# A dilated convolution: a shared middle-tap product, clipped columns, casting loads, stores from SyncE

## Chip, cores, metric

One core of one Trainium2 chip. The metric is the device time of one execution in microseconds (us). "Ratio" is the mean time of one kernel's fast runs over the mean of the kernel before's fast runs of the same rounds, so it is not quite the ratio of the medians quoted. Some runs fall in a slower state, in which the same kernel takes over 1.5% longer; all runs compared here are in the fast state unless said otherwise. A tile is a buffer on the chip; PSUM is the memory that TensorE writes its results to.

## The reference

```python
batch, c_in, h, w, c_out, k, dilation = 16, 64, 64, 64, 128, 3, 2   # x, weight: f32
x_pad = np.pad(x, ((0, 0), (0, 0), (2, 2), (2, 2)))
output[b, co] += weight[co, ci, kh, kw] * x_pad[b, ci, kh*2:kh*2+h, kw*2:kw*2+w]
```

So 16.8 MB of f32 images come in and 33.5 MB of f32 results go out. Output row r needs input rows r-2, r, r+2.

## The kernel before

Two images are worked on at once: their 64 input channels sit on partitions 0-63 and 64-127, and a pair of matmuls (one for each image) runs side by side on the two row halves of TensorE. Each output tile is 8 rows of 64 columns (512 numbers), and takes nine pairs, one for each tap. The parts that matter:

```python
    def emit_input_dma(pb):                      # f32 into a staging tile, from SyncE
        x32 = x32pool.tile([P, H, W], f32, tag="x32")
        for lo, hi in (chunk_rows0 if pb == 0 else chunk_rows):
            nc.sync.dma_start(out=x32[:, lo:hi], in_=x_pair[pb, :, lo:hi])
    def emit_cast(pb, lo, hi, engine):           # to f16 with 2 zero columns on each side
        ...  nc.vector.tensor_copy(out=x3[:, lo:hi, pad:pad+W], in_=x32[:, lo:hi, :])   # or nc.scalar.copy
    def conv_matmul(x3, ps, ti, t, hb, first, last):
        ...  # rows above or below the image are left out, columns are not
        rhs = x3[hb*CI:(hb+1)*CI, lo+dh:hi+dh, pad+dw:pad+dw+W]
        nc.tensor.matmul(out=po, lhsT=lhsT, rhs=rhs, start=first, stop=last)
    ...
        for ti in range(ntiles):                 # 8 tiles of 8 rows, 8 image pairs
            for t in range(ntaps):               # 9
                for hb in range(2):
                    conv_matmul(x3, ps, ti, t, hb, t == 0, t == ntaps - 1)
            ...  # ScalarE and VectorE copy one PSUM tile each into o_sb
            ...  # every 4th tile: nc.gpsimd.dma_start(out=out_img[...], in_=o_sb...)   1 MB each
```

## Time and profile before

| | before |
|---|---|
| time, median | 142.72 us (142.18 to 143.32, 4 runs) |
| span in the profile | 140.7 us |
| convolution matmuls, first start to last end | 10.6 to 134.2 us |
| last data packet of a store | 138.0 us |

Lines of the page of the kernel before: busy time by engine; busy tenths and GB/s in 40 slices of the span; the DMA queues (packets, MB, time of their packets as a share of 16 DMA engines).

```profile
span 140.7 us, 2777 instructions
...
PE 125.1 (89%) x1170; PEld 71.5 (51%) x1170; DVE 55.7 (40%) x85; ACT 53.8 (38%) x86; POOL 21.4 (15%) x49
...
PE   0049999999999999999999999999999999999910
...
DMA  4999999999999999999999999892929385799970
GB/s 97 296 415 418 415 401 414 344 428 418 424 422 422 428 417 425 429 411 424 425 424 423 422 421 428 354 414 121 426 100 431 165 356 245 298 395 402 388 307 8
...
q0 software_dynamic: 4816, 31.61, 54.3%
q1 hardware_dynamic: 5904, 18.88, 34.6%
```

TensorE is full from the fourth slice to the 38th. The DMA (16 engines that move the data in packets) is full as well, but only until about slice 26; the holes behind it (121, 100, 165 GB/s) say that DMA had time to spare. The two large queues together are 89% of the span, 125 us: the second limit lies right behind the first.

The same by stretches (columns: stretch, its length, busy us and count of instructions of each engine, granted clock, DMA share, GB/s):

```profile
core 0: us, PE busy (x) PEld busy (x) DVE busy (x) ACT busy (x) POOL busy (x), PEclk, DMA share, GB/s
30.00:60.00 30.00, 30.00 (x288) 17.18 (x285) 13.17 (x20) 12.45 (x21) 4.21 (x8) 1.00 1.02 423
100.00:110.00 10.00, 10.00 (x99) 5.80 (x96) 4.15 (x6) 3.35 (x6) 1.05 (x2) 1.00 0.75 312
```

Between 30 and 60 us loads and stores together move 423 GB/s at a share of 1.02 (60 to 90: 418): that is a full DMA (the share sums the times of packets, so packets that overlap bring it over 1). From 90 to 120 us, when the loads have run out, stores alone leave a quarter or more of it idle.

The timeline in the middle of the kernel, TensorE only (start us, length us, engine and what):

```profile
60.11 0.38 PE L133 MATMUL ps_732<-x_sb_78,w_sb 64*128 64x512 f16 x1
...
60.33 0.38 PE L133 MATMUL ps_732<-x_sb_78,w_sb 64*128 64x512 f16 x1
...
60.54 0.38 PE L133 MATMUL ps_732<-x_sb_78,w_sb 64*128 64x512 f16 x1
```

A new pair starts every 0.215 us (60.11, 60.33, 60.54): 512 columns, with nothing between. Nothing that leaves the matmul work as it is can shorten the stretch from 10.6 to 134.2 us.

### The profile page before, as it was taken

Reading aid. Unit: us, or ns where it says so; the run is one execution under the profiler, and the core shown is the slowest. Engines: PE = TensorE matmul, PEld = TensorE weight load, DVE = VectorE, ACT = ScalarE, POOL = GpSimd, SP = SyncE. Lnnn points to the kernel's source line nnn. Section 1 sums busy time; section 2 is a strip of 40 time slices with the busy share of each in tenths; the row PEclk is TensorE's granted clock in tenths of the full one; section 3 lists DMA queues with packets and bytes.
Section 4 is the critical chain, followed back from the end, with each engine's and each line's share of the span. In section 5 each row is a group of like instructions: output and inputs, shape, how many; then the busy total and the mean of one; then the engine's idle time right before and its main releaser. Section 6 shows DMA issues by size and latency. Waiting matters only on the chain.

```text
span 140.7 us, 2777 instructions
## 1 busy us (share of the span) xinstructions
PE 125.1 (89%) x1170; PEld 71.5 (51%) x1170; DVE 55.7 (40%) x85; ACT 53.8 (38%) x86; POOL 21.4 (15%) x49
## 2 busy tenths in 40 slices
PE   0049999999999999999999999999999999999910
PEld 0035555655555555655565555555565556555500
DVE  0134556535353534445353435333233333323310
ACT  3144465652535343533635253532233333322310
POOL 6000003020202020201102030202020110433210
PEclk9999999999999999999999999999999999999985
DMA  4999999999999999999999999892929385799970
GB/s 97 296 415 418 415 401 414 344 428 418 424 422 422 428 417 425 429 411 424 425 424 423 422 421 428 354 414 121 426 100 431 165 356 245 298 395 402 388 307 8
DMA packets 10733, 50.66 MB, mean 360 GB/s; under 512 B 1248, under 2 KB 1376, under 8 KB 7136
## 3 DMA queue, kind: packets, MB, share of 16 engines
q0 software_dynamic: 4816, 31.61, 54.3%
q1 hardware_dynamic: 5904, 18.88, 34.6%
q8 instruction: 9, 0.15, 0.4%
q14 instruction: 4, 0.03, 0.1%
HBM read 17.07 MB, written 33.55 MB: 360 GB/s over the span
## 4 chain that ended last, share of the span: by engine, by line
PE 73%; issue 12%; DMA 5%; POOL 3%; SPq 1%; ACT 1%; POOLq 0%
DMA x_87<-in_x_dram 5%; POOL out_dram L185 3%; PE ps_134 L133 1%; PE ps_1378 L133 1%; PE ps_1327 L133 1%; PE ps_1235 L133 1%; PE ps_1163 L133 1%; PE ps_1114 L133 1%; PE ps_1020 L133 1%; PE ps_972 L133 1%; PE ps_923 L133 1%; PE ps_829 L133 1%; PE ps_781 L133 1%; PE ps_732 L133 1%; PE ps_638 L133 1%
## 5 line engine op out<-in xcount | busy, mean ns | idle before, releaser
L133 PEld LDWEIGHTS <-w_sb 64*128 64x128 f16 x1152 | 70.2, 94 | 53.1 <-issue 1.1
L113 PE MATMUL wt_95<-ident,w_70 128*64 128x128 f16 x1 | 0.4, 377 | 7.7 <-DMA w_70<-in_weight_dram 7.7
L185 POOL DMA_DIRECT2D out_dram<-o_sb_1471 x8 | 4.3, 541 | 10.4 <-DVE o_sb_1471 L177 5.3
L100 DVE CAST x_sb_78<-x_87 128x640 f16<-128x640 f32 (+2 forms) x3 | 1.8, 606 | 8.9 <-DMA x_87<-in_x_dram 8.9
L113 PEld LDWEIGHTS <-w_70 128*64 128x64 f16 x9 | 1.1, 209 | 7.7 <-DMA w_70<-in_weight_dram 7.7
L185 POOL DMA_DIRECT2D out_dram<-o_sb_131 x2 | 1.1, 548 | 23.1 <-ACT o_sb_131 L180 19.3
L102 ACT CAST x_sb_78<-x_87 128x512 f16<-128x512 f32 (+1 forms) x2 | 1.7, 830 | 6.4 <-DMA x_87<-in_x_dram 6.4
L133 PE MATMUL ps_133<-x_sb_78,w_sb 64*128 64x512 f16 (+1 forms) x9 | 3.4, 557 | 0.0
L133 PE MATMUL ps_134<-x_sb_78,w_sb 64*128 64x512 f16 (+1 forms) x9 | 3.2, 528 | 0.0
L185 POOL DMA_DIRECT2D out_dram<-o_sb_898 x2 | 1.1, 532 | 13.1 <-ACT o_sb_898 L180 13.1
L185 POOL DMA_DIRECT2D out_dram<-o_sb_516 x2 | 1.1, 531 | 13.1 <-ACT o_sb_516 L180 13.1
L185 POOL DMA_DIRECT2D out_dram<-o_sb_707 x2 | 1.1, 531 | 13.1 <-ACT o_sb_707 L180 13.1
L185 POOL DMA_DIRECT2D out_dram<-o_sb_1089 x2 | 1.1, 531 | 13.1 <-ACT o_sb_1089 L180 13.1
L185 POOL DMA_DIRECT2D out_dram<-o_sb_325 x2 | 1.1, 531 | 13.1 <-DVE o_sb_326 L181 13.1
L185 POOL DMA_DIRECT2D out_dram<-o_sb_1280 x2 | 1.1, 531 | 12.8 <-ACT o_sb_1280 L180 12.8
L102 ACT CAST x_sb_84<-x_391 128x1024 f16<-128x1024 f32 (+1 forms) x2 | 2.0, 992 | 2.6 <-DMA x_391<-in_x_dram 2.6
L102 ACT CAST x_sb_81<-x_200 128x1024 f16<-128x1024 f32 (+1 forms) x2 | 2.0, 990 | 2.6 <-DMA x_200<-in_x_dram 2.6
L102 ACT CAST x_sb_78<-x_582 128x1024 f16<-128x1024 f32 (+1 forms) x2 | 2.0, 994 | 1.4 <-PE ps_255 L133 1.4
L100 DVE CAST x_sb_84<-x_391 128x1152 f16<-128x1152 f32 (+1 forms) x2 | 1.5, 727 | 2.4 <-DMA x_391<-in_x_dram 2.4
L102 ACT CAST x_sb_81<-x_773 128x1024 f16<-128x1024 f32 (+1 forms) x2 | 2.0, 993 | 0.9 <-PE ps_423 L133 0.9
L102 ACT CAST x_sb_78<-x_1155 128x1024 f16<-128x1024 f32 (+1 forms) x2 | 2.0, 994 | 0.9 <-PE ps_805 L133 0.9
L102 ACT CAST x_sb_81<-x_1346 128x1024 f16<-128x1024 f32 (+1 forms) x2 | 2.0, 994 | 0.9 <-PE ps_996 L133 0.9
(309 smaller groups left out, 373.2 us busy)
## 6 DMA issues: line engine op xcount, KB each, us to landing
out_dram<-o_sb_131 POOLq DMA_DIRECT2D x2, 1024.0 KB, 10.3
out_dram<-o_sb_132 POOLq DMA_DIRECT2D x2, 1024.0 KB, 13.0
out_dram<-o_sb_325 POOLq DMA_DIRECT2D x2, 1024.0 KB, 11.1
out_dram<-o_sb_326 POOLq DMA_DIRECT2D x2, 1024.0 KB, 14.3
out_dram<-o_sb_516 POOLq DMA_DIRECT2D x2, 1024.0 KB, 11.1
out_dram<-o_sb_517 POOLq DMA_DIRECT2D x2, 1024.0 KB, 14.4
out_dram<-o_sb_707 POOLq DMA_DIRECT2D x2, 1024.0 KB, 10.8
out_dram<-o_sb_708 POOLq DMA_DIRECT2D x2, 1024.0 KB, 13.4
```

What stands on the lines that cost most here:

```text
L100: nc.vector.tensor_copy(out=x3[:, lo:hi, pad : pad + W], in_=x32[:, lo:hi, :])
L102: nc.scalar.copy(out=x3[:, lo:hi, pad : pad + W], in_=x32[:, lo:hi, :])
L113: nc.tensor.matmul(out=wt_ps[0:CI, 0:CO], lhsT=w_slice, rhs=ident)
L133: nc.tensor.matmul(out=po, lhsT=lhsT, rhs=rhs, start=first, stop=last)
L185: nc.gpsimd.dma_start(out=out_img[2 * pb, :, e0:e1], in_=o_sb0[:, e0:e1])
```

## The change

The intent: rows are taken in blocks of four. With a = rows 4b, 4b+1 and c = rows 4b+2, 4b+3 (c' the same of the block above, a' of the block below) and W0, W1, W2 the three rows of taps, output rows a need W1·a + W2·c + W0·c', and output rows c need W1·c + W0·a + W2·a'. The product W1·(a + c) is made once and added to both; the rest becomes (W2 - W1)·c + W0·c' and (W0 - W1)·a + W2·a'. That is five products instead of six. Side taps work on the 62 columns that exist. GpSimd's software queue casts f32 to f16 while loading, so the f32 staging and the casts on VectorE and ScalarE go. Stores are issued by SyncE; the instruction order is by hand.

```diff
-            nc.sync.dma_start(out=x32[:, lo:hi], in_=x_pair[pb, :, lo:hi])
-            nc.vector.tensor_copy(out=x3[:, lo:hi, pad : pad + W], in_=x32[:, lo:hi, :])
+        nc.gpsimd.dma_start(out=x16_tiles[pb][...], in_=x_pair[pb, :, lo:hi])      # f32 -> f16, 16-row chunks
+        nc.vector.tensor_tensor(out=s, in0=v[:, :, 0], in1=v[:, :, 1], op=add)      # rowsum: a + c
...
-            for t in range(ntaps):
-                for hb in range(2):
-                    conv_matmul(x3, ps, ti, t, hb, t == 0, t == ntaps - 1)
+            o0, o1 = max(0, -dw), W - max(0, dw)                                     # clipped columns
+        product(psP, sv, 0, 0, NBLK, True, True)                                     # W1 (a + c)
+        product(psA, blocks(x16, b0, NBLK, 1), 1, 0, NBLK, True, False)              # (W2 - W1) c
+        product(psA, blocks(x16, b0 + z - 1, NBLK - z, 1), 2, z, NBLK - z, False, True)   # W0 c'
+        product(psB, blocks(x16, b0, NBLK, 0), 3, 0, NBLK, True, False)              # (W0 - W1) a
+        product(psB, blocks(x16, b0 + 1, NBLK - z, 0), 4, 0, NBLK - z, False, True)  # W2 a'
...
-                nc.vector.tensor_copy(out=o_sb0[:, sl], in_=ps[0])
-                nc.scalar.copy(out=o_sb1[:, sl], in_=ps[1])
+        nc.scalar.copy(out=p_sb, in_=psP)
+        for e, ps in ((0, psA), (1, psB)):
+            nc.vector.tensor_tensor(out=o[...], in0=ps..., in1=pv, op=add)
...
-                nc.gpsimd.dma_start(out=out_img[2 * pb, :, e0:e1], in_=o_sb0[:, e0:e1])
+                nc.sync.dma_start(out=out_img[2 * pb + m, :, e0:e1], in_=o_tiles[pb][...])
... (weights cast and subtracted on VectorE/ScalarE, pools and order left out)
```

A "group" below is 16 rows of two images: 15 matmul pairs where there were 18.

More of the change, by code (lines that the diff above doesn't have):

```diff
@@ L22 @@
     CO, CI_w, KH, KW = weight.shape
-    assert CI == CI_w
-    d = 2 if isinstance(dilation, bass.AP) else int(dilation)
-    assert KH == KW == 3
-    assert CI == 64 and CO == 128
+    assert CI == CI_w == 64 and CO == 128
+    assert KH == KW == 3 and H == W == 64
     assert B % 2 == 0
+    assert not isinstance(dilation, bass.AP) and int(dilation) == 2
+    d = 2
     P = 128
-    pad = d
-    WP = W + 2 * pad
-    HW = H * W
     f32 = mybir.dt.float32
     f16 = mybir.dt.float16
-    ROWS = 512 // W
@@ L38 @@
-    ntiles = H // ROWS
-    assert H % ROWS == 0
-    NB = ROWS * W
-    CR = 2 * ROWS
-    nchunks = ntiles // 2
-    chunk_rows = [(0, CR + d)]
-    for c in range(1, nchunks - 1):
-        chunk_rows.append((c * CR + d, (c + 1) * CR + d))
-    chunk_rows.append(((nchunks - 1) * CR + d, H))
-    assert nchunks == 4
-    chunk_rows0 = [(0, ROWS + d), (ROWS + d, CR + d)] + chunk_rows[1:]
-    taps = [(0, 0)]
-    for kh in range(KH):
-        for kw in range(KW):
-            dh = (kh - KH // 2) * d
-            dw = (kw - KW // 2) * d
-            if (dh, dw) != (0, 0):
-                taps.append((dh, dw))
@@ L58 @@
-    ntaps = len(taps)
+    add = mybir.AluOpType.add
+    sub = mybir.AluOpType.subtract
+    HW = H * W
+    GR = 16
+    NG = H // GR
+    NBLK = GR // 4
+    NH = GR // 2 * W
     npairs = B // 2
-    NXB = 3
+    ngroups = npairs * NG
+    chunk_rows = [(g * GR + (d if g else 0), min((g + 1) * GR + d, H)) for g in range(NG)]
+    LOOK = 3
+    XB = 10
     wpool = ctx.enter_context(tc.tile_pool(name="wpool", bufs=1))
-    x32pool = ctx.enter_context(tc.tile_pool(name="x32pool", bufs=2))
-    xpool = ctx.enter_context(tc.tile_pool(name="xpool", bufs=1))
@@ L66 @@
-    opool = ctx.enter_context(tc.tile_pool(name="opool", bufs=4))
-    cpool = ctx.enter_context(tc.tile_pool(name="cpsum", bufs=8, space=bass.MemoryType.PSUM))
-    w16 = wpool.tile([CO, CI * KH * KW], f16, name="w16")
-    nc.gpsimd.dma_start(out=w16, in_=weight.rearrange("o i h w -> o (i h w)"))
+    xpool = ctx.enter_context(tc.tile_pool(name="xpool", bufs=5))
+    opool = ctx.enter_context(tc.tile_pool(name="opool", bufs=3))
+    spool = ctx.enter_context(tc.tile_pool(name="spool", bufs=3))
@@ new lines, with load @@
+    ppool = ctx.enter_context(tc.tile_pool(name="ppool", bufs=1, space=bass.MemoryType.PSUM))
+    apool = ctx.enter_context(tc.tile_pool(name="apool", bufs=3, space=bass.MemoryType.PSUM))
+    x_pair = x.rearrange("(nb two) c h w -> nb (two c) h w", two=2)
+    out_img = out.rearrange("b o h w -> b o (h w)")
+    x16_tiles = {}
+    xs_tiles = {}
+    def load(c):
+        pb, g = divmod(c, NG)
+        lo, hi = chunk_rows[g]
+        if g == 0:
+            x16_tiles[pb] = xpool.tile([P, HW], f16, tag="x16", name="x16")
+            xs_tiles[pb] = xpool.tile([P, HW // 2], f16, tag="xs", name="xs")
+        nc.gpsimd.dma_start(
+            out=x16_tiles[pb][:, lo * W : hi * W].rearrange("p (h w) -> p h w", w=W),
+            in_=x_pair[pb, :, lo:hi],
+        )
@@ new lines, in rowsum @@
+    def rowsum(c):
+        pb, g = divmod(c, NG)
+        v = x16_tiles[pb][:, g * GR * W : (g + 1) * GR * W].rearrange(
+            "p (b e q) -> p b e q", e=2, q=2 * W
+        )
+        s = xs_tiles[pb][:, g * NH : (g + 1) * NH].rearrange("p (b q) -> p b q", q=2 * W)
+        nc.vector.tensor_tensor(out=s, in0=v[:, :, 0], in1=v[:, :, 1], op=add)
+    ctx.enter_context(tc.manual_schedule())
+    w32 = wpool.tile([CO, CI * KH * KW], f32, name="w32")
+    nc.scalar.dma_start(out=w32, in_=weight.rearrange("o i h w -> o (i h w)"))
@@ L72 @@
     ident = wpool.tile([P, P], f16, name="ident")
     make_identity(nc, ident)
-    w_sb = wpool.tile([P, ntaps * CO], f16, name="w_sb")
-    x3_bufs = []
-    for i in range(NXB):
-        x_sb = xpool.tile([P, H * WP], f16, tag=f"xsb{i}", name=f"x_sb{i}")
-        x3 = x_sb.rearrange("p (h w) -> p h w", w=WP)
-        nc.gpsimd.memset(x3[:, :, 0:pad], 0.0)
-        nc.gpsimd.memset(x3[:, :, pad + W :], 0.0)
-        x3_bufs.append(x3)
-    x_pair = x.rearrange("(nb two) c h w -> nb (two c) h w", two=2)
@@ L86 @@
-    out_img = out.rearrange("b o h w -> b o (h w)")
-    x32_tiles = {}
-    def emit_input_dma(pb):
-        x32 = x32pool.tile([P, H, W], f32, tag="x32")
-        x32_tiles[pb] = x32
-        for lo, hi in (chunk_rows0 if pb == 0 else chunk_rows):
-            nc.sync.dma_start(out=x32[:, lo:hi], in_=x_pair[pb, :, lo:hi])
-    def emit_cast(pb, lo, hi, engine):
-        x3 = x3_bufs[pb % NXB]
-        x32 = x32_tiles[pb]
-        if engine == "v":
-            nc.vector.tensor_copy(out=x3[:, lo:hi, pad : pad + W], in_=x32[:, lo:hi, :])
-        else:
-            nc.scalar.copy(out=x3[:, lo:hi, pad : pad + W], in_=x32[:, lo:hi, :])
@@ L104 @@
-    emit_input_dma(0)
-    emit_cast(0, chunk_rows0[0][0], chunk_rows0[0][1], "v")
-    emit_cast(0, chunk_rows0[1][0], chunk_rows0[1][1], "s")
-    for t, (dh, dw) in enumerate(taps):
-        kh = dh // d + KH // 2
-        kw = dw // d + KW // 2
-        w_slice = w16.rearrange("o (i k) -> o i k", k=KH * KW)[:, :, kh * KW + kw]
-        wt_ps = cpool.tile([CO, NB], f32, tag="ps", name=f"wt{t}")
-        nc.tensor.matmul(out=wt_ps[0:CI, 0:CO], lhsT=w_slice, rhs=ident)
-        nc.tensor.matmul(out=wt_ps[CI : 2 * CI, 0:CO], lhsT=w_slice, rhs=ident)
-        dst = w_sb[:, t * CO : (t + 1) * CO]
-        if t % 2 == 0:
-            nc.scalar.copy(out=dst, in_=wt_ps[:, 0:CO])
-        else:
-            nc.vector.tensor_copy(out=dst, in_=wt_ps[:, 0:CO])
@@ L121, in conv_matmul @@
-    def conv_matmul(x3, ps, ti, t, hb, first, last):
-        dh, dw = taps[t]
-        r0 = ti * ROWS
-        lo = max(r0, -dh)
-        hi = min(r0 + ROWS, H - dh)
-        lhsT = w_sb[hb * CI : (hb + 1) * CI, t * CO : (t + 1) * CO]
-        rhs = x3[
-            hb * CI : (hb + 1) * CI,
-            lo + dh : hi + dh,
-            pad + dw : pad + dw + W,
-        ]
-        po = ps[hb][:, (lo - r0) * W : (hi - r0) * W]
-        nc.tensor.matmul(out=po, lhsT=lhsT, rhs=rhs, start=first, stop=last)
@@ L135 @@
-    for pb in range(npairs):
-        x3 = x3_bufs[pb % NXB]
-        o_sb0 = opool.tile([P, HW], f32, tag="osb")
-        o_sb1 = opool.tile([P, HW], f32, tag="osb")
-        first_pair = pb == 0
-        last_pair = pb == npairs - 1
-        if last_pair:
-            flush_after = {ti: (ti * NB, (ti + 1) * NB) for ti in range(ntiles)}
-        else:
-            flush_after = {
-                ntiles // 2 - 1: (0, HW // 2),
-                ntiles - 1: (HW // 2, HW),
-            }
-        for ti in range(ntiles):
-            ps = [
-                cpool.tile([CO, NB], f32, tag="ps", name=f"ps{hb}") for hb in range(2)
-            ]
-            for t in range(ntaps):
-                for hb in range(2):
-                    conv_matmul(x3, ps, ti, t, hb, t == 0, t == ntaps - 1)
-            if first_pair:
-                if ti == 0:
-                    emit_cast(0, chunk_rows[1][0], chunk_rows[1][1], "v")
-                    emit_cast(0, chunk_rows[2][0], chunk_rows[2][1], "s")
-                elif ti == 1:
-                    emit_cast(0, chunk_rows[3][0], chunk_rows[3][1], "v")
-            if pb + 1 < npairs:
-                if ti == 2:
-                    emit_input_dma(pb + 1)
-                elif ti == 4:
-                    emit_cast(pb + 1, chunk_rows[0][0], chunk_rows[0][1], "v")
-                    emit_cast(pb + 1, chunk_rows[1][0], chunk_rows[1][1], "s")
-                elif ti == 5:
-                    emit_cast(pb + 1, chunk_rows[2][0], chunk_rows[2][1], "v")
-                    emit_cast(pb + 1, chunk_rows[3][0], chunk_rows[3][1], "s")
-            sl = slice(ti * NB, (ti + 1) * NB)
-            if ti % 2 == 0:
-                nc.vector.tensor_copy(out=o_sb0[:, sl], in_=ps[0])
-                nc.scalar.copy(out=o_sb1[:, sl], in_=ps[1])
-            else:
-                nc.scalar.copy(out=o_sb0[:, sl], in_=ps[0])
-                nc.vector.tensor_copy(out=o_sb1[:, sl], in_=ps[1])
-            if ti in flush_after:
-                e0, e1 = flush_after[ti]
-                nc.gpsimd.dma_start(out=out_img[2 * pb, :, e0:e1], in_=o_sb0[:, e0:e1])
-                if last_pair:
-                    nc.sync.dma_start(
-                        out=out_img[2 * pb + 1, :, e0:e1], in_=o_sb1[:, e0:e1]
-                    )
-                else:
-                    nc.gpsimd.dma_start(
-                        out=out_img[2 * pb + 1, :, e0:e1], in_=o_sb1[:, e0:e1]
-                    )
@@ new lines @@
+    for c in range(XB):
+        if c < ngroups:
+            load(c)
+    KINDS = 5
+    wd = wpool.tile([CO, KINDS * KW * 2 * CI], f16, name="wd")
+    wdv = wd.rearrange("o (k j r i) -> o k j r i", k=KINDS, j=KW, r=2)
+    wv = w32.rearrange("o (i h w) -> o h w i", h=KH, w=KW)
+    for r in range(2):
+        nc.vector.tensor_copy(out=wdv[:, 0, :, r], in_=wv[:, 1])
+        nc.vector.tensor_tensor(out=wdv[:, 1, :, r], in0=wv[:, 2], in1=wv[:, 1], op=sub)
+        nc.vector.tensor_tensor(out=wdv[:, 3, :, r], in0=wv[:, 0], in1=wv[:, 1], op=sub)
+        nc.scalar.copy(out=wdv[:, 2, :, r], in_=wv[:, 0])
+        nc.scalar.copy(out=wdv[:, 4, :, r], in_=wv[:, 2])
@@ new lines @@
+    w_sb = wpool.tile([P, KINDS * KW * CO], f16, name="w_sb")
+    NT = KINDS * KW
+    for q in range(0, NT, 8):
+        n = min(8, NT - q)
+        wt = apool.tile([P, 1024], f32, tag="ab", name="wt")
+        for t in range(q, q + n):
+            nc.tensor.matmul(
+                out=wt[:, (t - q) * CO : (t - q + 1) * CO],
+                lhsT=wd[:, t * 2 * CI : (t + 1) * 2 * CI],
+                rhs=ident,
+            )
+        h = n // 2 * CO
+        nc.vector.tensor_copy(out=w_sb[:, q * CO : q * CO + h], in_=wt[:, 0:h])
+        nc.scalar.copy(out=w_sb[:, q * CO + h : (q + n) * CO], in_=wt[:, h : n * CO])
@@ new lines, in product @@
+    def product(ps, src, kind, blk0, nblk, first, last):
+        for j in (1, 0, 2):
+            dw = (j - 1) * d
+            o0, o1 = max(0, -dw), W - max(0, dw)
+            t = kind * KW + j
+            for hb in range(2):
+                pp = slice(hb * CI, (hb + 1) * CI)
+                rhs = src(pp, dw + o0, dw + o1)
+                po = ps[:, hb * NH + blk0 * 2 * W : hb * NH + (blk0 + nblk) * 2 * W]
+                po = po.rearrange("p (r w) -> p r w", w=W)[:, :, o0:o1]
+                nc.tensor.matmul(
+                    out=po,
+                    lhsT=w_sb[pp, t * CO : (t + 1) * CO],
+                    rhs=rhs,
+                    start=first and j == 1,
+                    stop=last and j == 2,
+                )
@@ new lines, in blocks, with prepare @@
+    def blocks(x16, b0, n, e):
+        v = x16.rearrange("p (b e r w) -> p b e r w", e=2, r=2, w=W)
+        return lambda pp, c0, c1: v[pp, b0 : b0 + n, e, :, c0:c1]
+    ahead = [0]
+    def prepare(n):
+        while ahead[0] < min(n, ngroups):
+            c = ahead[0]
+            rowsum(c)
+            if c + XB < ngroups:
+                load(c + XB)
+            ahead[0] += 1
+    prepare(2)
+    o_tiles = {}
+    for G in range(ngroups):
+        pb, g = divmod(G, NG)
+        x16 = x16_tiles[pb]
+        xs = xs_tiles[pb].rearrange("p (r w) -> p r w", w=W)
+        if g == 0:
+            o_tiles[pb] = opool.tile([P, 2 * HW], f32, tag="osb", name="osb")
+        o = o_tiles[pb].rearrange("p (m b e q) -> p m b e q", m=2, e=2, q=2 * W)
+        b0 = g * NBLK
+        psP = ppool.tile([P, 2 * NH], f32, tag="p", name="psP")
+        sv = lambda pp, c0, c1: xs[pp, g * GR // 2 : (g + 1) * GR // 2, c0:c1]
+        product(psP, sv, 0, 0, NBLK, True, True)
+        psA = apool.tile([P, 2 * NH], f32, tag="ab", name="psA")
+        product(psA, blocks(x16, b0, NBLK, 1), 1, 0, NBLK, True, False)
+        z = 1 if g == 0 else 0
+        product(psA, blocks(x16, b0 + z - 1, NBLK - z, 1), 2, z, NBLK - z, False, True)
+        psB = apool.tile([P, 2 * NH], f32, tag="ab", name="psB")
+        product(psB, blocks(x16, b0, NBLK, 0), 3, 0, NBLK, True, False)
+        z = 1 if g == NG - 1 else 0
+        product(psB, blocks(x16, b0 + 1, NBLK - z, 0), 4, 0, NBLK - z, False, True)
+        p_sb = spool.tile([P, 2 * NH], f32, tag="psb", name="p_sb")
+        nc.scalar.copy(out=p_sb, in_=psP)
+        pv = p_sb.rearrange("p (m b q) -> p m b q", m=2, q=2 * W)
+        for e, ps in ((0, psA), (1, psB)):
+            nc.vector.tensor_tensor(
+                out=o[:, :, b0 : b0 + NBLK, e],
+                in0=ps.rearrange("p (m b q) -> p m b q", m=2, q=2 * W),
+                in1=pv,
+                op=add,
+            )
+        prepare(min(2 * G + 4, G + 1 + LOOK))
+        if g % 2 == 1:
+            e0, e1 = (g - 1) * GR * W, (g + 1) * GR * W
+            for m in range(2):
+                nc.sync.dma_start(
+                    out=out_img[2 * pb + m, :, e0:e1],
+                    in_=o_tiles[pb][:, m * HW + e0 : m * HW + e1],
+                )
```

## The prediction

> **What bounds the kernel now.** TensorE does. In the timeline a pair of convolution matmuls (two images on the two row halves, 512 columns) starts every 0.216 us, from 10.6 to 134 us without a gap; the page's part 1 has PE busy 125.1 us of a span of 140.7. The last stores end 6.5 us later. Right behind stands the DMA: page part 3 gives its two large queues 54.3% and 34.6% of the span, 125 us together; the slices show it full until about 85 us (423 GB/s), with holes only after the loads have run out.
>
> **What the change does.**
> - TensorE: per 16 rows 15 pairs for 18, and side taps of 62 columns for 64. Columns per image pair fall 19%, from 36,096 to 29,328. At the 0.216 us per 512 columns of the trace the convolution takes 99-100 us (3.1 us per 16-row group) for 123. I expect no penalty for 62-column rows.
> - Casts leave VectorE and ScalarE, about 25 us each. VectorE gets per group two PSUM additions of 1,024 and a row sum of 512. The trace's 512-element PSUM copy took 0.692 us, 0.53 of it streaming; I estimate 2.65 us per group, 85 us in all: below TensorE. ScalarE: one copy of 1,024, about 1.0 us.
> - DMA: HBM bytes stay, 17.07 MB in and 33.55 out. Stores move to SyncE, which buys no bandwidth: the Trainium skill ("DMA: Bandwidth & Descriptors", "Issuing engines are not separate DMA queues") says all issuers share 16 engines, and the packet records agree: 4 KB rows take 159-162 ns on either queue. An 8 KB store row takes 309 ns; 256 such per engine are 79 us. For the cast there is one sample: the weights (2,304 B read, 1,152 written per row) took 106 ns a row. A plain row of that size would take about 93 by the other rows (9 ns + 27.3 B/ns). So a cast is charged for the bytes it reads, plus 12-15%. Plain 4 KB load rows take 159 ns; cast I estimate 171-183, so 44-47 us for all loads.
>
> **Critical path.** DMA work becomes 79 + 44..47 + about 2 (weights, semaphores, instruction fetch) = 125-128 us, more than TensorE's 99-100: the bound moves to DMA, and only part of the 23 us is collected. The first x packet comes later: GpSimd issues it after the identity, about 1.9 us, and that queue's first packet came 2.8 us after its issue in before, so at 4.7 us; before, loads began at 1.8. The DMA ends near 130 us; plus 2.7 us of ending as in before and 2 us between span and time: about **134.5 us**, range 128 to 139.5.
>
> Chances: over 2% faster 0.87, within 2% 0.10, slower 0.03.
>
> **What would show it.** DMA nines from slice 2 to the end; the software queue shows about 8.5 MB (it counts written bytes) yet 31-35% of the span, the hardware queue 33.6 MB and 58%; the last matmul ends near 110 us, then 15-20 us of pure stores; matmul pairs at about 0.21 us; cast rows of 2 KB at 171-183 ns; the chain ends in DMA.
>
> **What would make it wrong.** A cast cheaper than its read bytes (written-byte cost: about 125 us) or much dearer (over 140). Strided 62-column PSUM rows slowing matmuls by over 20%. Loads starved by 8 KB store rows, or the three output buffers stalling VectorE, so that TensorE ends late and DMA idles.

## The result, and the profile after

130.77 us median (130.54 to 130.93, 4 runs), before 142.72; ratio 0.9169 (95% interval 0.9131 to 0.9208). The prediction was 134.5 us with a range of 128 to 139.5.

The page of the changed kernel (parts 1 to 4, the lines that answer to those above, and the chain):

```profile
span 129.1 us, 2299 instructions
...
PE 103.4 (80%) x975; PEld 53.8 (42%) x975; DVE 91.4 (71%) x104; ACT 36.7 (28%) x39; POOL 17.7 (14%) x38
...
PE   0469999999999999999999999999999998000000
...
DMA  3999999999999999999999999999999999999980
GB/s 101 147 183 173 204 208 263 348 344 362 333 346 350 351 346 335 348 349 343 354 335 345 346 358 346 342 342 353 364 405 430 416 432 419 432 427 427 432 353 38
...
q1 hardware_dynamic: 4608, 33.56, 63.2%
q0 software_dynamic: 4608, 8.39, 35.9%
...
PE 79%; DVE 3%; DMA 2%; DVEq 1%; issue 0%
```

DMA nines now run to slice 38 without a hole, and TensorE stops at slice 34. With the weights' queue (0.7%) and the two instruction queues (0.3%) the page's queues sum to 100% of the span. Note the GB/s line: the page counts a casting load by the bytes that it writes, half of those that it reads. A slice with 345 GB/s, 69 of them cast, reads and writes 414.

```profile
core 0: us, PE busy (x) PEld busy (x) DVE busy (x) ACT busy (x) POOL busy (x), PEclk, DMA share, GB/s
30.00:60.00 30.00, 30.00 (x296) 15.62 (x292) 26.35 (x30) 9.80 (x10) 4.22 (x8) 1.00 1.05 345
110.00:120.00 10.00, 0.00 (x0) 0.00 (x0) 0.72 (x1) 0.00 (x0) 0.00 (x0) 0.58 1.01 428
```

TensorE stays full while it works (30.00 of 30 us), DMA too (share 1.05). From 110 us on, only stores run, at 428 GB/s.

The timeline in the middle, matmuls merged by tile:

```profile
40.18 1.23 DVE L190 TENSOR_TENSOR osb<-psA,p_sb 128x1024 f32<-128x1024 f32 x1 [0.42 <-PE psA L136]
41.16 0.81 PE L136 MATMUL psP<-xs,w_sb 64*128 64x512 f16 x6
41.38 1.23 DVE L190 TENSOR_TENSOR osb<-psB,p_sb 128x1024 f32<-128x1024 f32 x1
...
42.52 0.41 DVE L87 TENSOR_TENSOR xs<-x_174 128x512 f16<-128x512 f16 x1
...
44.34 0.81 PE L136 MATMUL psP<-xs,w_sb 64*128 64x512 f16 x6
```

psP starts at 41.16 and the next psP at 44.34: a group takes 3.17-3.18 us for 15 pairs, 0.211 us a pair. VectorE's two additions and the row sum fill 2.8 of them (1.23 + 1.22 + 0.42, the second following the first by 1.20).

The chain of waits, last pieces (start, length, what):

```profile
106.99 1.28 PE psA L136 x12
108.37 1.23 DVE osb L190
109.59 1.13 DVEq L236
```

The last matmul ends at 109.4 us; the chain ends with VectorE's last addition at 110.7 us and gives TensorE 79% of the span. But the span ends at 129.1 us. The 18 us in between are stores that nothing but the end of the program waits for, and the chain does not follow them. Which of the two pictures bounds the kernel is the first thing that the experiments asked.

The balance of the change in the two profiles: the convolution begins 2.7 us earlier (7.9 for 10.6) and is 22.1 us shorter (101.5 for 123.6), so the last matmul ends 24.8 us earlier (109.4 for 134.2). After the last matmul come 19.7 us for 6.5, so 13.2 us are given back. 24.8 - 13.2 = 11.6 us, the difference of the spans (140.7 - 129.1).

The packet records of the trace, which the page sums up, in medians of one data packet and in bytes counted at the source:

| | before | after |
|---|---|---|
| x row of 16 image rows: read -> written, ns | 4,096 -> 4,096 B: 159 | 4,096 -> 2,048 B: 172 |
| store row 8,192 B, ns | 309 | 322 beside casts, 309 alone |
| first x packet, us | 1.76 | 2.87 |
| GB/s read and written, 30-60 us | 423 | 414 |
| GB/s read and written, 5-15 us | 409-414 | 366 |
| last data packet, us | 138.0 | 127.4 |
| span end after it, us | 2.7 | 1.7 |

### The profile page after: what moved, and what is told of

The parts are those of the page before. It is cut to its first block, busy times and chain, and to the rows that moved or that the text cites. A ratio compares the mean times of both kernels' runs of the same rounds, so it can differ in the third digit from the quotient of the medians.

```text
span 129.1 us, 2299 instructions
## 1 busy us (share of the span) xinstructions
PE 103.4 (80%) x975; PEld 53.8 (42%) x975; DVE 91.4 (71%) x104; ACT 36.7 (28%) x39; POOL 17.7 (14%) x38
## 3 DMA queue, kind: packets, MB, share of 16 engines
q1 hardware_dynamic: 4608, 33.56, 63.2%
q0 software_dynamic: 4608, 8.39, 35.9%
## 4 chain that ended last, share of the span: by engine, by line
PE 79%; DVE 3%; DMA 2%; DVEq 1%; issue 0%
PE psA L136 31%; PE psB L136 30%; PE psP L136 16%; DMA w_75<-in_weight_dram 2%; PE wt L116 1%; DVE osb L190 1%; DVEq L236 1%; DVE wd L105 1%; DVE w_sb L122 0%; DVE wd L107 0%; DVE wd L106 0%; DVE xs L87 0%; DVEq L190 0%
## 5 line engine op out<-in xcount | busy, mean ns | idle before, releaser
L136 PEld LDWEIGHTS <-w_sb 64*128 64x128 f16 x960 | 52.3, 95 | 50.0 <-issue 3.0
L187 ACT COPY p_sb<-psP 128x1024 f32<-128x1024 f32 x32 | 32.4, 1012 | 67.6 <-PE psP L136 67.6
L190 DVE TENSOR_TENSOR osb<-psA,p_sb 128x1024 f32<-128x1024 f32 x32 | 39.2, 1225 | 14.3 <-PE psA L136 13.6
L190 DVE TENSOR_TENSOR osb<-psB,p_sb 128x1024 f32<-128x1024 f32 x32 | 39.1, 1222 | 0.6 <-PE psB L136 0.6
L136 PE MATMUL psP<-xs,w_sb 64*128 64x496 f16 (+1 forms) x192 | 26.5, 379 | 1.0 <-DVE xs L87 1.0
L136 PE MATMUL psA<-x_82,w_sb 64*128 64x496 f16 (+3 forms) x48 | 6.7, 421 | 0.0
L136 PE MATMUL psB<-x_82,w_sb 64*128 64x496 f16 (+3 forms) x48 | 6.3, 400 | 0.0
L116 PE MATMUL wt<-ident,wd 128*128 128x128 f16 x15 | 1.9, 311 | 5.0 <-DVE wd L105 5.0
L136 PE MATMUL psA<-x_786,w_sb 64*128 64x496 f16 (+3 forms) x48 | 5.6, 365 | 0.0
L136 PE MATMUL psA<-x_88,w_sb 64*128 64x496 f16 (+3 forms) x48 | 5.6, 365 | 0.0
L136 PE MATMUL psA<-x_297,w_sb 64*128 64x496 f16 (+3 forms) x48 | 5.6, 365 | 0.0
L136 PE MATMUL psA<-x_460,w_sb 64*128 64x496 f16 (+3 forms) x48 | 5.6, 365 | 0.0
L136 PE MATMUL psA<-x_94,w_sb 64*128 64x496 f16 (+3 forms) x48 | 5.6, 365 | 0.0
L136 PE MATMUL psA<-x_174,w_sb 64*128 64x496 f16 (+3 forms) x48 | 5.6, 365 | 0.0
L136 PE MATMUL psA<-x_623,w_sb 64*128 64x496 f16 (+3 forms) x48 | 5.6, 365 | 0.0
L136 PE MATMUL psB<-x_88,w_sb 64*128 64x496 f16 (+3 forms) x48 | 5.6, 365 | 0.0
L136 PE MATMUL psB<-x_94,w_sb 64*128 64x496 f16 (+3 forms) x48 | 5.6, 365 | 0.0
L136 PE MATMUL psB<-x_297,w_sb 64*128 64x496 f16 (+3 forms) x48 | 5.6, 365 | 0.0
L136 PE MATMUL psB<-x_460,w_sb 64*128 64x496 f16 (+3 forms) x48 | 5.6, 365 | 0.0
L136 PE MATMUL psB<-x_786,w_sb 64*128 64x496 f16 (+3 forms) x48 | 5.6, 365 | 0.0
L136 PE MATMUL psB<-x_174,w_sb 64*128 64x496 f16 (+3 forms) x48 | 5.6, 365 | 0.0
L136 PE MATMUL psB<-x_623,w_sb 64*128 64x496 f16 (+3 forms) x48 | 5.6, 365 | 0.0
```

The source lines that it names most:

```text
L116: nc.tensor.matmul(out=wt[:, (t - q) * CO : (t - q + 1) * CO], lhsT=wd[:, t * 2 * CI : (t + 1) * 2 * CI], rhs=ident,)
L136: nc.tensor.matmul(out=po, lhsT=w_sb[pp, t * CO : (t + 1) * CO], rhs=rhs, start=first and j == 1, stop=last and j == 2,)
L187: nc.scalar.copy(out=p_sb, in_=psP)
L190: nc.vector.tensor_tensor(out=o[:, :, b0 : b0 + NBLK, e], in0=ps.rearrange("p (m b q) -> p m b q", m=2, q=2 * W), in1=pv, op=add,)
```

## The experiments

Theory: the 16 DMA engines bound the changed kernel, from the first x packet to the last store. First rival: TensorE still does, as the chain has it. Further rivals concern what the cast, the issuing engines and the early stretch are worth.

### pe_light: six of fifteen matmul pairs taken out (wrong result)

```diff
-        product(psA, blocks(x16, b0 + z - 1, NBLK - z, 1), 2, z, NBLK - z, False, True)
-        product(psB, blocks(x16, b0 + 1, NBLK - z, 0), 4, 0, NBLK - z, False, True)
... (and stop=True on the product before each)
```

> Wrong result on purpose: the second product of each output half is left out (9 matmul pairs per group for 15), everything else as in the changed kernel. Theory (the 16 DMA engines bound the changed kernel, 124.5 us of them end to end): no change, 130.0 to 131.5 us, last matmul near 100 us, the rest stores. Rival (the chain of waits is right when it gives TensorE 79%): the matmul stretch shrinks to VectorE's 2.8 us per group, about 90 us, and the time falls to about 122 us.

Measured: 130.99 us (130.70 to 131.45), ratio 0.9194. Of its page, the busy line, TensorE and DMA in 40 slices, and the chain:

```profile
PE 70.2 (54%) x591; PEld 35.4 (27%) x591; DVE 88.3 (68%) x104; ACT 36.7 (28%) x39; POOL 17.7 (14%) x38
...
PE   0369988688868886855665544666544570000000
...
DMA  3899999999999999999999999999999999999970
...
DMA 71%; DVE 4%; issue 4%; POOL 3%; DVEq 1%; POOLq 0%
```

TensorE works 33 us less (70.2 busy for 103.4) and the time stays. The DMA row is nearly the same as in the changed kernel, and the chain now gives the DMA 71% (waits for x chunks) where it gave TensorE 79%, for the same time. The rival falls: TensorE's 79% in the chain is not what the time hangs on. (The last matmul ended at 106.3 us, where I had expected 100: VectorE's row sums waited 14 times for an x chunk, 14.6 us in all, so late in the kernel the DMA set TensorE's pace as well.)

### no_shared: the shared product undone, all else kept

```diff
-        product(psP, sv, 0, 0, NBLK, True, True)
-        product(psA, blocks(x16, b0, NBLK, 1), 1, 0, NBLK, True, False)
+        product(psA, blocks(x16, b0, NBLK, 0), 0, 0, NBLK, True, False)
+        product(psA, blocks(x16, b0, NBLK, 1), 1, 0, NBLK, False, False)
... (the same for psB; weights not subtracted; no row sum, no p_sb; one copy on ScalarE, one on VectorE; 4 PSUM buffers for 3 + 1)
```

> The shared product undone (18 pairs per group for 15, no row sum, evacuation by one ScalarE and one VectorE copy); cast loads, SyncE stores, clipped columns and order kept. Right result. Theory (the gain comes from taking TensorE below the DMA work): convolution 120.7 us from about 7.5 us, so last matmul at 128 us, then one copy and the last 2 MB of stores, span about 136.5, time 138 us (136 to 140). Rival (the gain comes from the loads by casting DMA, the early start and the stores, not from the product): within 1.5 us of 130.8 us.

Measured: three fast runs 139.18, 139.52 and 141.18 us (mean 140.0), and a slow one of 143.32; ratio of the fast runs 0.9823 (0.9745 to 0.9901). The profile fell in the slow run, whose matmul pairs took 0.220 us, so only its pattern is read (TensorE and DMA in 40 slices of its page):

```profile
PE   0599999999999999999999999999999999999400
...
DMA  4999999999999999999999999999776583929294
```

Here TensorE is full to the end and the DMA has holes, as in before. (unclip_ns below, whose profile is of a fast run, shows the same pattern.) Added to the kernel before, the casting loads, the earlier start, clipping and SyncE stores together are thus worth 2.6 us (142.6 to 140.0, in the same rounds; 1.4 to 3.6 by the interval of the ratio); the shared product, added last, brings the other 9.2 us (140.0 to 130.8). In another order the split could differ, since what a part is worth hangs on the limit; that was not run. The product could have brought more: 32 groups times three pairs of 0.211 us are 20.3 us of TensorE time. The rest went where the DMA took over.

### f32_loads and pool_stores: loads without the cast; stores in the loads' queue

f32_loads loads plain f32 from SyncE into 8 staging buffers, casts on ScalarE, and stores from GpSimd. To make room, loads run 8 chunks ahead for 10, and there are 3 x buffers for 5; both hold for f32_hw too.

```diff
-        nc.gpsimd.dma_start(out=x16_tiles[pb][...], in_=x_pair[pb, :, lo:hi])
+        st = stpool.tile([P, (GR + d) * W], f32, tag="st", name="st")               # 8 buffers
+        nc.sync.dma_start(out=st[...], in_=x_pair[pb, :, lo:hi])
+        nc.scalar.copy(out=x16_tiles[pb][...], in_=st_tiles.pop(c)[...])             # before its rowsum
-                nc.sync.dma_start(out=out_img[2 * pb + m, :, e0:e1], ...)
+                nc.gpsimd.dma_start(out=out_img[2 * pb + m, :, e0:e1], ...)
```

> The changed kernel with plain f32 loads from SyncE into 8 staging buffers, casts on ScalarE (about 1.0 us each, 32), stores from GpSimd. Right result. Theory (DMA bound, a cast row occupies an engine longer than a plain row, and the software queue starts 1.1 us later): DMA from 1.8 us at the 421 GB/s of before, done at 121 to 123 us, time 125 us (124 to 128). Rival 1 (a cast row costs no throughput because packets overlap): 129 to 130 us, only the start is gained. Rival 2 (TensorE bounds): 130 to 132 us.

Measured: 133.30 us (132.45 to 134.09), ratio 0.9355 (0.9295 to 0.9414). A miss: neither 125 nor 130. DMA started at 1.74 us and did run at 421-423 GB/s from 30 to 90 us, as expected, but only at 350-380 from 15 to 30 us, so that the last packet came at 127.8 us, no earlier than in the changed kernel; and the span ended 2.6 us after it, for 1.7. f32_hw below moves the stores back to SyncE (and the later loads to ScalarE's queue), which leaves the first of these to be seen by itself.

pool_stores only changes the issuer of the stores in the changed kernel:

```diff
-                nc.sync.dma_start(out=out_img[2 * pb + m, :, e0:e1], ...)
+                nc.gpsimd.dma_start(out=out_img[2 * pb + m, :, e0:e1], ...)
```

> The changed kernel with its stores from GpSimd, in the queue of the loads. Theory (all issuers share the 16 engines; the issuer buys no bandwidth): 130 to 132.5 us. Rival (two queues that alternate are what fills the engines): 134 us or more, since loads then wait behind stores and packets overlap less.

Measured: 133.90 us (133.76 to 134.63), ratio 0.9408 (0.9367 to 0.9449): 3.1 us slower than the changed kernel, a miss for the theory as I had put it. The profiles split it: the last data packet comes 0.9 us later (128.25 for 127.39), and the span ends 3.75 us after it, for 1.7. Throughput from 60 to 90 us was 421 GB/s counted at the source, not lower than the changed kernel's 416; from 30 to 60 us it was 405 for 414. So the larger part of what SyncE's stores are worth is not bandwidth. It is how soon the program ends after the last byte. The instruction records show where: the last transfer is reported landed at 128.6 us and SyncE is done at 128.8, but GpSimd's closing instruction, a DRAIN, ends only at 131.3 us, 3.0 us after its queue's last data packet. In the changed kernel that DRAIN ends 2.0 us after the last packet of the loads (98.96 for 96.95 us), long before the stores are through, and costs nothing.

### f32_hw: plain loads again, stores from SyncE

```diff
+        (nc.sync if c < XB else nc.scalar).dma_start(out=st[...], in_=...)           # first 8 loads SyncE, later ScalarE
+                nc.sync.dma_start(out=out_img[2 * pb + m, :, e0:e1], ...)
```

> As f32_loads (plain f32 loads, casts on ScalarE), but stores from SyncE as in the changed kernel and the later loads from ScalarE's queue: what the cast in the DMA is worth with the end of the kernel kept alike. Theory (the cast costs 1.5 to 2% of the mixed stretch, 415 against 421-423 GB/s, and f32_loads lost by the late end of software stores, 2.6 us after the last packet for 1.7): 129.5 us (128 to 131), at or just below the changed kernel. Rival (staging buffers hold loads back early on, as at 20 to 30 us in f32_loads, and that is what cost it): 132 us or more again.

Measured: 132.15 us (131.82 to 132.63), ratio 0.9244 (0.9203 to 0.9284). The span now ended 1.4 us after the last packet (129.4 us), so the late end is gone; the kernel is still 1.4 us slower than with casting loads. The windows (columns as before: stretch, length, PE, PEld, DVE, ACT, POOL, clock, DMA share, GB/s):

```profile
15.00:20.00 5.00, 5.00 (x46) 2.38 (x42) 3.99 (x6) 2.52 (x3) 0.00 (x0) 1.00 0.87 343
20.00:25.00 5.00, 5.00 (x52) 2.54 (x48) 4.17 (x6) 3.52 (x4) 0.00 (x0) 1.00 0.93 352
30.00:60.00 30.00, 30.00 (x294) 15.54 (x290) 26.35 (x31) 19.14 (x20) 0.00 (x0) 1.00 1.02 418
```

At 15 to 25 us the DMA share is 0.87-0.93: it has gaps, while the changed kernel's windows of these 10 us show 1.06 and more. A further load is issued only after the cast that frees a staging buffer. That cast stands on ScalarE behind the copy of psP, which waits for TensorE, so from 15 us the trace has one load per group, 3.1 to 3.7 us apart (issues at 15.5, 19.2, 22.3, 25.4 us), where 0.5 MB at 420 GB/s take 1.25 us; the first store packet comes only at 21.9 us (21.4 in the changed kernel). Over 15 to 30 us f32_hw moved 5.1 MB and the changed kernel 6.3 MB (GB/s by window, at the source); the 1.2 MB are 2.8 us at 420 GB/s, more than the whole loss. The rival holds in part: the gaps, 0.15 and 0.09 of two stretches of 5 us below the 1.02 of a full DMA, are 1.2 us or 0.5 MB of it. What plain loads would win in the mixed stretch (418 for 414 here) is too little to pay for that. The rest stays open: packets took longer. From 25 to 30 us the share was 1.00 at only 329 GB/s; store rows averaged 396 ns (median 313) and 4 KB load rows 201 ns (median 159), and no run tells why. So it isn't shown that deeper staging alone would make plain loads the faster ones. The changed kernel's early stretch has such packets too (5 to 10 us: 4 KB rows average 194 ns, median 173).

### dma_only and dma_plain: the transfers by themselves (wrong result)

dma_only keeps all loads and stores and drops all computing; dma_plain makes the loads plain.

```diff
-    (weights, products, additions; 8 x buffers for 5)
+    nc.vector.memset(o, 1.0)            # one tile, stored again and again by nc.sync.dma_start
-        nc.gpsimd.dma_start(...)         # dma_plain only: into f32 tiles
+        nc.scalar.dma_start(...)
```

> Wrong result on purpose: all loads (casting, GpSimd) and all stores (SyncE, of one constant tile) of the changed kernel, with no computing but one fill of that tile. Theory (the DMA itself is the floor of the changed kernel): last packet at 126 to 128 us, time 129 to 131.5 us although nothing waits for TensorE, VectorE or a load. Rival (stalls between compute and DMA cost it something): under 127 us.

> Wrong result on purpose: the same with the loads plain f32 from ScalarE's queue. Theory (a cast row costs little throughput: 415 against 422 GB/s where mixed, and the start is 1.1 us earlier): 2 to 3.5 us less than dma_only. Rival (by packet times, 172 against 159 ns a row, nothing hidden): 4.5 us or more less. Second rival (cast is free): only the 1.1 us of the start.

Measured: dma_only 130.86 us (130.69 to 131.08), ratio 0.9178 (0.9121 to 0.9236); dma_plain has three fast runs, 127.05, 127.20 and 128.92 us (mean 127.7), and a slow one of 130.52; ratio of the fast runs 0.8957 (0.8872 to 0.9042). From dma_only's page the span and the DMA slices, then the windows from 30 to 60 us, first of dma_only, then of dma_plain (stretch, length, VectorE, GpSimd, clock, DMA share, GB/s):

```profile
span 129.1 us, 121 instructions
...
DMA  3999999999999999999999999999999999999981
```

```profile
30.00:60.00 30.00, 0.00 (x0) 4.22 (x8) 1.00 1.05 348
```

```profile
30.00:60.00 30.00, 0.00 (x0) 0.00 (x0) 1.00 1.02 423
```

Without a single matmul the transfers of the changed kernel take 130.86 us, and with all its computing 130.77. This is the strongest evidence for the theory: computing adds nothing that shows, and the last packet (127.4 us in both) is the DMA's own. That they agree to 0.1 us is partly chance, for the order differs: dma_only's stores begin at 13.4 us for 21.4, its loads last until 113.6 us for 97.0, and 5 to 10 us ran at 347 GB/s for 366. The cast: by packet times a row takes 8% longer (172 for 159 ns), but the share of 1.05 for 1.02 says that packets of the cast kernel overlap more. At the source dma_only moved 417 GB/s in this window, and dma_plain 423, 1.4% more. The 3.2 us between the means of the fast runs (130.9 and 127.7) are inside the 2 to 3.5 expected, but dma_plain's fast runs scatter over 1.9 us, so the size is rough. The first x packet (2.96 us for 2.88) did not come earlier here; ScalarE had issued the weights first. The profile of dma_plain is of its slowest fast run, 2.0 us shorter than dma_only's: the last packet came 1.5 us earlier (125.9 for 127.4), nearly all of it rate, and the span ended 1.2 us after it for 1.7. The rate gained in the mixed stretch and from 5 to 10 us (401 for 347 GB/s), and lost from 10 to 15 us (344 for 363).

### hybrid: first six chunks plain, the others cast

```diff
+        if c < NF:                                                                   # NF = 6
+            nc.sync.dma_start(out=st[...], in_=x_pair[pb, :, lo:hi])                 # 6 staging buffers, each used once
+            return
         nc.gpsimd.dma_start(out=x16_tiles[pb][...], in_=x_pair[pb, :, lo:hi])
...
+            if 0 < c < NF:
+                cast(c)                                                              # nc.scalar.copy, f32 -> f16
... (identity made after GpSimd's first loads; 4 x buffers for 5)
```

> The changed kernel with its first six chunks loaded as plain f32 from SyncE and cast on ScalarE, the other 26 by casting DMA; identity made after the first loads. Right result. Theory (DMA bound, so only an earlier first packet and a fuller early stretch can gain: first packet at 1.75 us for 2.87, 412 GB/s for 366 at 5 to 15 us): 1 to 2 us less than the changed kernel, 129 us. Rival (the end is set by something else, the last stores for instance): no change.

Measured: 128.91 us (128.55 to 129.16, 6 runs), ratio 0.9024 (0.8996 to 0.9052), correct. It beats both kernels: 0.9024 / 0.9169 is 1.6% less time than the changed one. Its windows (GB/s again with cast loads counted by written bytes; at the source 401 and 413):

```profile
5.00:10.00 5.00, 1.87 (x15) 1.53 (x16) 3.36 (x8) 3.26 (x6) 1.56 (x4) 1.00 1.06 318
10.00:15.00 5.00, 4.40 (x24) 1.99 (x25) 1.63 (x4) 4.54 (x6) 0.66 (x2) 1.00 1.09 308
```

The first x packet came at 1.77 us, and 5 to 15 us moved 401-413 GB/s for 366. The last packet came at 126.07 us, 1.3 us earlier, and the span ended 1.3 us after it for 1.7 (together the 1.7 us between the spans), although TensorE began later (its busy time in these 10 us is 6.3 us for 9.0) and its last matmul ended at 112.0 us for 109.4. A kernel that computes later and ends sooner is bound by what it moves. Which of the two, first packet or early rate, gave how much was not separated.

### load_first: two loads ahead of the identity

```diff
-    make_identity(nc, ident)
     for c in range(XB):
         load(c)
+        if c == 1: make_identity(nc, ident)
```

> The changed kernel with two loads issued before the identity is made, 0.65 us earlier. Theory (every microsecond by which the DMA starts later is paid in full): 0.5 to 0.7 us less than the changed kernel, about 130.2 us. Rival (the early stretch is slow anyway, 230 GB/s until 5 us, and eats it): no change within 0.3 us.

Measured: 130.13 us (129.78 to 130.72, 6 runs), ratio 0.9112 (0.9081 to 0.9143). The median is 0.64 us lower, as expected, but not for the reason given: the trace shows the first load issued at 1.23 us for 1.41, and its first packet at 2.79 for 2.87. The start moved by 0.1-0.2 us, not 0.65. The stretch from 5 to 15 us ran at 384-386 GB/s for 366, and the last packet came 0.7 us earlier, in one profile of each. The intervals of the two ratios also overlap. I count this run as inconclusive.

### unclip and unclip_ns: all 64 columns (wrong result)

```diff
-            o0, o1 = max(0, -dw), W - max(0, dw)
+            o0, o1 = 0, W
```

> Wrong result on purpose: the changed kernel with all taps on all 64 columns (side taps unshifted). A pair of side-tap matmuls should take 0.2155 us for the clipped 0.209, a group 3.23 us for 3.17, the last matmul end 2 us later (110.3 us). Theory (TensorE is off the critical path): time within 0.5 us of the changed kernel, 130.3 to 131.3 us. Rival (TensorE is on it, as the chain of waits says): 2 us more, 132.8 us.

> Wrong result on purpose: no_shared with all taps on all 64 columns. There TensorE bounds the time: 384 side-tap pairs at 16 columns of 0.4 ns less clipping, so about 2.5 us more than no_shared's fast runs (mean 140.0 us): 142.5 us (141.5 to 143.5).

Measured: unclip 130.94 us (130.75 to 131.31), ratio 0.9180, a group 3.24 us for 3.17, convolution 104.2 us long for 101.5, last matmul at 112.5 us (I had expected 110.3); unclip_ns 141.59 us (141.16 to 142.43), ratio 0.9924 (0.9871 to 0.9976). In the changed kernel clipping saves TensorE 2.7 us and the time nothing that shows (130.94 for 130.77, ranges overlapping). In no_shared, which TensorE bounds, the medians and means say about 1.6 us (141.6 for fast runs of 140.0, in another job; 1.0% by the ratios) where I expected 2.5. But the two intervals overlap, so this is not clear of noise. Run against run at like granted clock the direction is the same: 141.2 and 141.2 us for 139.2 and 139.5 at 0.985-0.986, 142.0 and 142.4 for 141.2 at 0.977. That the same edit is worth something or nothing by where the limit lies is thus shown for the nothing, and only indicated for the something.

## Why the prediction was right

- **What bounded the kernel before, and that the bound would move to the DMA: right.** For the new bound pe_light, unclip and dma_only each show it without the others. "Only part of the 23 us is collected": TensorE's stretch shrank by 22.1 us, the time by 12.0.
- **TensorE: right.** 101.5 us and 3.17 us a group for "99-100 us (3.1 us per 16-row group)", last matmul at 109.4 us for "near 110". No penalty for 62 columns: a group of 15 pairs, ten of them clipped, starts 3.171 us after the one before, and in unclip 3.237, so a clipped pair is 6.6 ns shorter; 16 columns at 2.4 GHz (TensorE's full clock in the Trainium skill, "TensorE: Matmul & The Clock Gate", "What's actually happening") are an estimated 6.7 ns. (The lengths of single matmuls in a trace are modelled, so starts are compared.)
- **VectorE: a little low.** 91.4 us busy for 85. (The casts that left were also smaller than "about 25 us each": 12.0 us on VectorE and 15.6 us on ScalarE in the trace of before. VectorE stayed below TensorE, so neither mattered.)
- **The cast row: right in its time, too dear in its effect.** Medians of 172 and 153-191 ns for 4 KB and the other row sizes, in the range of "171-183" for 4 KB rows; it is charged for the bytes that it reads. But the queues' packet times sum to 129 us, more than the 125 to 128 predicted, and fit into 124.5 us from first x packet to last, because packets overlap (share 1.05 in place of the 1.01-1.02 of before). The rate at the source fell by 1-2%, not by the 8% that the packet time suggests. Nor is the surcharge a percentage: it is 13 ns for every row size (93 to 106, 140 to 153, 159 to 172, 178 to 191 ns), and it isn't the cast row's alone. In hybrid the plain 4 KB rows took 159 ns until the first cast packet and 172 after it, and store rows from SyncE took 322 ns beside casts for 309, while in pool_stores store rows in the casts' own queue kept 309. Here the sum of packet times was an upper estimate of what a cast costs. That 124.5 us came so near the 125.3 of the forecast (4.7 to 130 us) is partly luck: the slower store rows (322 for 309 ns beside casts) made the sum larger than predicted, and the overlap, which the prediction did not have, took more than that away.
- **The first packet: the term that was off most.** "at 4.7 us" was 2.87 us. I had estimated an issue at 1.9 us and a delay of 2.8 us, from a single DMA of before. Measured: issue at 1.41 us, delay 1.46 us. This is 1.8 of the 3.7 us between forecast and result. The sample of before was issued while SyncE's loads were already running; hybrid has such a case too, and there the delay was 4.3 us (1.22 to 5.54). Where no x load ran yet, it was 1.45 to 1.74 us in all eight traces with that queue alone at first. So the sample was not like the case; that the running loads are the cause was not tested by itself.
- **The end: 1.2 us.** I kept 2.7 us of ending and 2 us between span and time from before; they were 1.7 and 1.8. "Stores move to SyncE, which buys no bandwidth" holds for bandwidth and missed this: with the stores in the software queue pool_stores ends 3.75 us after its last packet, against 1.7. The sum: 2.87 + 124.5 + 1.7 + 1.8 = 130.9, for 4.7 + 125.3 + 2.7 + 2 = 134.7 by the prediction's terms (it rounded to 134.5).
- **Signs: one of them wrong.** "The chain ends in DMA" did not show; the chain stopped at VectorE's last addition. DMA nines without holes, 15-20 us of pure stores, 8.4 MB of the software queue at 35.9% (said: 31-35) and 33.6 MB of the hardware queue at 63.2% (said: 58) did show; both shares are higher since the span is shorter and store rows next to casts take 322 ns for 309.

## What to carry to other kernels

When one engine is the limit, look for the second limit before cutting the first: here the queues' packet times (125 us) gave a fair estimate in advance of how much of a 23 us saving could be kept. The chain of waits here followed instructions and ended at 110.7 us; the 18 us of stores after it belonged to the DMA, however large TensorE's share of the chain was. Such a stretch is a sign to test for: taking work out of the suspected engine, or keeping the transfers alone, settled it here in one run each. Once the DMA was the limit, what still moved the time in these runs was an earlier first packet and a fuller early stretch (hybrid), the rate of the transfers themselves (dma_plain), and a queue that ends soon after its last byte (pool_stores).

## What the Trainium skill lacked or had wrong

- "DMA: Bandwidth & Descriptors", "Issuing engines are not separate DMA queues": it says that another issuer only saves issue time. The mixed rates agree (60 to 90 us: 421 GB/s with all in one queue, 416 with two), but stores from GpSimd made the kernel 3.1 us slower than stores from SyncE; 2 us of it lie between the last data packet and the end of the span (3.75 us for 1.7), where GpSimd's closing DRAIN ends 3.0 us after the last packet. The page does not mention this.
- The same page, "Specifications", gives first-byte latencies of about 1 us for the software path and 0.6 us for the hardware path. It does not say from where they count. Counted from the end of the issuing instruction they agree with the changed kernel: 0.64 us for the hardware issue of the weights (1.10 to 1.74) and 0.8 us for the first software issue (2.07 to 2.87). Counted from its start they are 1.0 and 1.5 us. For a software issue beside running loads the page has no figure: 2.2 us from its end in the kernel before (1.93 to 4.09), 3.7 in hybrid (1.89 to 5.54).
- No page gives the cost of a cast in a DMA. Here: 172 ns for a row of 4 KB read and 2 KB written, against 159 plain, and the same 13 ns more for rows of 2.3 to 4.6 KB; 417 GB/s against 423 at the source with stores running beside it.
- "PSUM — Partial Sum Buffer", "Specifications (TRN2)", says that a non-contiguous access pattern slows matmuls significantly. Rows of 62 out of 64 f32 columns did not: a pair of 496 columns took 6.6 ns less than one of 512 (groups of 3.171 and 3.237 us).
